# Streamed weights split by transfers: a rounding one for the first part, a negation on ACT, an adding one for the second

## The chip, the cores and the metric

The kernel runs on one core of a Trainium2 chip. The metric is the device time of one execution in microseconds (us), lower is better. Engines: TensorE (PE in the rows; PEld is its loading of weights), VectorE (DVE), ScalarE (ACT), GpSimd (POOL) and SyncE (SP), which issues transfers. SPq, POOLq and so on are the engines' queues.

## The reference

One step of a two-layer backbone with 512 latent and 128 context tokens, width 1024:

```
for l in range(2):
    mp, ms = modulation(c_ctx, ...), modulation(c, ...)     # silu(c) @ w_mod + b_mod, six parts
    h = rmsnorm(x, g_norm1) * (1 + m[1]) + m[0]
    qa, ka, va, qb, kb, vb, qc, kc, vc, gates = split(h @ w_in)     # 1024 -> 6912
    oa = diff_attention(...)            # 4 heads of two maps
    ob = gqa_attention(...)             # 8 heads on 2 key heads
    oc = neighbourhood_attention(...)   # 8 heads, latents; dense for the context
    y = g0 * (oa @ w_branch_a) + g1 * (ob @ w_branch_b) + g2 * (oc @ w_branch_c)
    x = x + m[2] * (y @ w_out)
    h2 = rmsnorm(x, g_norm2) * (1 + m[4]) + m[3]
    x = x + m[5] * (square(relu(h2 @ w_ff1)) @ w_ff2)       # 1024 -> 4096 -> 1024
y = rmsnorm(x, g_final)
```

Everything is float32; the new keys and values of the context are returned too.

## The kernel before

All 640 tokens stand as columns in on-chip memory. A float32 product is computed as three products of the faster fp32r type: both operands are split into a first part (rounded to fp32r) and a second (what is left), and first x first, first x second and second x first are summed. The two halves of the tokens are 256 and 384 columns (`HALVES`), so a block of 128 x 128 weights takes six matmuls.

**Stages of a layer.** First ten *units* of the mixer (`Unit`, u = 0 to 3 kind A, 4 and 5 kind B, 6 to 9 kind C): a unit projects the tokens with eight pieces of 384 weight columns (five token tiles, eight pieces, three matmuls each: 120 matmuls) and does its attention, whose steps are interleaved with the next unit's projections. Then gates and branches (three times eight gate products and eight branch products), then the out projection (its last part token half by token half, with the norm behind it: `staggered`), then the MLP in groups of blocks (`ff1`, `ff2`, `ff1_pair`), whose hidden pairs use a product scheme with seven summands made from sums of weights.

**The weights** are one long stream in HBM (`_stream`), cut into items by `_program`: kind "n" (loads of 768 columns, used as pieces of 384), kind "m" (512 or 256 columns, the second MLP product) and kind "s" (the seven summands of a hidden pair, made by sums of four loads). `Stream.make` prepares items ahead of their use: a load by SP into `raws` (or `spare`), the first part by ACT (`act(hi, x, AF.Copy)`, a rounding copy), the second by a subtraction, on POOL while `self.lo` is "POOL" (the units, `pl.ptt`), on VectorE after (`tt`). Both parts lie in rings `whis` and `wlos` of 10 x 384 columns; a place is refilled after the last matmul that reads it. In the units `ws.hold` keeps all eight pieces of a unit until its last token tile, which leaves two places for the next unit.

**The order.** Nothing is issued as the program is written. `Plan` records every operation with its engine, an assumed duration and its dependencies; `Plan.schedule` then runs a list scheduler over the records (each engine takes the earliest written operation that is ready) and `Plan.issue` writes the engines' programs in that order, which is fixed from then on: an engine that waits holds up all that stands behind it in its queue. Recorded helpers all have one line each: L245 matmul, L248 transpose, L262 ACT, L267 most of DVE, L280 a fused DVE operation, L294 the modulation's dot products, L305 and L311 POOL's one- and two-operand operations, L317 SP's transfers. Names in the rows: mf and mr are the large memories of float32 and fp32r, psm the accumulators, U, U1A, U1B, U1C further memories, w the weight stream, wmod the modulation weights, ospill the spilled branch outputs.

Of the kernel before, what the change touches and what calls it, by code (L numbers as in the profile page):

```python
# [13 lines left out]
AF = mybir.ActivationFunctionType  # L14
ALU = mybir.AluOpType
# [33 lines left out]
def f32(ap):  # L49
    return ap.bitcast(F32)  # L50
# [7 lines left out]
class Plan:  # L58
# [211 lines left out]
    def tt(self, out, a, b, op):  # L270
        self.vec("tensor_tensor", out, (a, b), op)
# [41 lines left out]
    def dma(self, out, in_, keys_out=(), keys_in=()):  # L313
# [2 lines left out]
            nb *= c  # L316
        self.add("SP", 60, lambda R: self.nc.sync.dma_start(R(out), R(in_)), [out], [in_], keys_out, keys_in, nbytes=4 * nb)  # L317


class Slots:  # L320

# [140 lines left out]
def hybrid_plan(pl, a, mf, mr, view, psm, xspill, ospill):  # L462
    mm, tp, act, tt, ts, stt = pl.mm, pl.tp, pl.act, pl.tt, pl.ts, pl.stt
# [43 lines left out]
    class Banks:  # L507
        def __init__(self, ids, w=1):
            self.ids, self.w, self.i = ids, w, 0
# [25 lines left out]
    class Stream:  # L535
# [3 lines left out]
        def __init__(self):  # L539
            self.items = []  # L540
            off = 0
            home = False
            for kind, n in _program():
                if kind == "layer":
                    home = True
                elif kind == "n":
                    c = 0
                    while c < n:
                        w = min(CW, n - c)
                        for j in range(0, w, PW):  # L550
                            self.items.append(("n", off, w, j, min(PW, w - j), home))
                            home = False
                        off += P * w
                        c += w
                elif kind == "m":
                    self.items.append(("m", off, n, 0, n, False))
                    off += P * n
                else:
                    self.items.append(("s", off, 0, n, SW, False))
                    if n == 0:  # L560
                        off += 4 * P * SW
            self.raws, self.parts = Circle(3 * CW), Circle(10 * PW)
            self.made = self.cur = self.off = 0
            self.hold = None
            self.pieces, self.v0 = {}, {}
            self.lo = "DVE"
            self.sum1 = self.spare = None

        def load(self, off, w):
# [8 lines left out]
        def make(self, upto):  # L578
            while self.made < min(upto, len(self.items)):
                i = self.made  # L580
                kind, off, w, j, n, home = self.items[i]
                if home:
                    self.parts.home()
                end = self.parts.look(n) + n
                h = self.cur if self.hold is None else self.hold
                if h in self.v0 and end - self.v0[h] > self.parts.size:
                    assert i > self.cur
                    break
                if kind == "n":
                    if j == 0:  # L590
                        self.raw = self.load(off, w)
                    x = self.raw[:, j:j + n]
                elif kind == "m":
                    x = self.spare.get()[:, :n]
                    pl.dma(x, self.piece(off, n))
                else:
                    if j == 0:
                        self.q = [self.load(off + k * P * SW, SW) for k in range(4)]
                    q, s1 = self.q, self.sum1
                    if j == 2:  # L600
                        tt(s1, q[2], q[3], ALU.add)
                        tt(q[2], q[0], q[2], ALU.subtract)
                        tt(q[0], s1, q[0], ALU.subtract)
                    if j == 6:
                        tt(q[1], q[1], q[0], ALU.subtract)
                    x = (q[0], q[1], q[0], s1, q[2], q[3], q[1])[j]
                self.v0[i], b = self.parts.take(n)
                hi, lo = whis[:, b:b + n], wlos[:, b:b + n]
                act(hi, x, AF.Copy)
                if self.lo == "POOL":  # L610
                    pl.ptt(lo, x, f32(hi), ALU.subtract)
                else:
                    tt(lo, x, f32(hi), ALU.subtract)
                self.pieces[i] = (hi, lo)
                self.made += 1
# [10 lines left out]
    ws = Stream()  # L626
# [667 lines left out]
    for l in range(DEPTH):  # L1294
# [11 lines left out]
        n = 0  # L1306
        for u in range(NU):
            un = Unit(l, u, ph)
            un.cached()
            if l == 0 and u == 0:  # L1310
                for t in ORDER:
                    un.evacuate(first_z[t], t)
            else:
                ws.hold = ws.cur
                W = [ws.get(UW, 1) for _ in range(KT)]
                ws.hold = None
                for t in ORDER:
                    un.project(W, t)
            for job in un.jobs():
                jobs.append(job)  # L1320
                step(n)
                n += 1
# [395 lines left out]
```

## Time and profile before

| | |
|---|---|
| median of 3 runs | 2417.46 us (2413.13 to 2419.87) |
| profiled execution | 2413.36 us |
| its span, first to last instruction | 2411.3 us |
| granted TensorE clock, mean | 0.99 |
| TensorE busy | 2330.3 us (97%) |
| VectorE / ACT / POOL busy | 1854.2 / 1227.5 / 445.3 us |
| moved by transfers | 245.39 MB |

Busy time is the time in which an engine executes something; waiting and issuing of transfers don't count. The rows below come from one execution, the profiled one. In a row of groups, the first figures are the busy time and the mean duration of one, and behind the second bar stands how long the engine was idle just before them and what ended it.

### The profile page before, as it was taken

How to read it: one execution, taken by the hardware profiler on the slowest of the kernel's cores; microseconds unless marked ns; L12 is line 12 of the kernel's file. 1: busy time of each engine (PE TensorE's matmuls, PEld its weight loads, DVE VectorE, ACT ScalarE, POOL GpSimd, SP SyncE). 2: the span in 40 equal slices, each digit the busy share in tenths (PEclk: the TensorE clock that was granted, in tenths of full speed). 3: DMA queues.
4: the chain of work that ended last, by engine and by line, in shares of the span. 5: the costliest groups of instructions: out<-in, count | busy, mean ns of one | idle time of the engine just before them, and what ended most of it. 6: DMA issues, size and time to landing. Idle time of an engine off the chain costs nothing. (4 is left out here: it accounts for less than half of the span.)

```text
span 2411.3 us, 42109 instructions
## 1 busy us (share of the span) xinstructions
PE 2330.3 (97%) x15460; PEld 2257.2 (94%) x15460; DVE 1854.2 (77%) x4067; ACT 1227.5 (51%) x2838; POOL 445.3 (18%) x527
## 2 busy tenths in 40 slices
PE   7898999999999899999999999999999999999997
PEld 5798999999999899999989998999999999999997
DVE  6878878789746999877787787777983688767777
ACT  4556677642233644444476567775222364444443
POOL 4636533300000000000034455431000000000000
PEclk8999999999999999999999999999999999999999
DMA  6211112476422244322241112226662212322222
GB/s 243 88 49 59 52 46 87 130 234 220 137 77 72 66 140 131 103 82 84 75 134 55 51 48 66 66 93 223 205 201 80 77 53 75 85 83 80 80 75 66
DMA packets 107346, 245.39 MB, mean 102 GB/s; under 512 B 13058, under 2 KB 26882, under 8 KB 106116
## 3 DMA queue, kind: packets, MB, share of 16 engines
q1 hardware_dynamic: 107140, 242.71, 32.6%
q8 instruction: 121, 1.98, 0.3%
q14 instruction: 85, 0.70, 0.1%
HBM read 225.62 MB, written 17.04 MB: 101 GB/s over the span
## 5 line engine op out<-in xcount | busy, mean ns | idle before, releaser
L245 PE MATMUL psm<-mr 128*128 128x256 f32 (+2 forms) x10688 | 1792.4, 319 | 21.0 <-ACT mr L262 8.8
L245 PEld LDWEIGHTS psm<-mr 128*128 128x128 f32 x10688 | 1640.6, 189 | 32.3 <-ACT mr L262 12.0
L262 ACT ACTIVATE mr<-mf 128x384 fp32r<-128x384 f32 (+4 forms) x948 | 470.6, 516 | 661.6 <-PE psm L245 576.9
L267 DVE TENSOR_TENSOR mr<-mf,mr 128x384 fp32r<-128x384 f32 (+5 forms) x780 | 432.1, 566 | 166.2 <-ACT mr L262 161.4
L280 DVE SCALAR_TENSOR_TENSOR mf<-psm,mf 128x256 f32<-128x256 f32 (+2 forms) x628 | 228.1, 408 | 92.9 <-PE psm L245 83.0
L311 POOL TENSOR_TENSOR mr<-mf,mr 128x384 fp32r<-128x384 f32 (+1 forms) x168 | 188.9, 1144 | 474.0 <-ACT mr L262 466.4
L262 ACT ACTIVATE mf<-mf 128x320 f32<-128x320 f32 (+6 forms) x417 | 195.9, 489 | 97.3 <-DVE mf L267 51.8
L311 POOL TENSOR_TENSOR mf<-mf 128x256 f32<-128x256 f32 (+3 forms) x93 | 89.9, 967 | 826.8 <-DVE mf L267 806.1
L294 DVE CUSTOM_DVE_ANT_0 psm<-mf,U1B 128x1024 f32<-128x1024 f32 x160 | 198.6, 1241 | 17.0 <-DMA mf<-wmod 15.8
L305 POOL TENSOR_SCALAR mf<-mf 128x640 f32<-128x640 f32 (+3 forms) x236 | 144.7, 617 | 350.9 <-DVE mf L267 284.1
L262 ACT ACTIVATE mf<-psm,mf 128x640 f32<-128x640 f32 (+3 forms) x256 | 162.4, 643 | 65.8 <-DVE mf L267 48.3
L245 PE MATMUL psm<-U,mr 128*128 128x320 f32 (+1 forms) x1176 | 186.4, 305 | 5.2 <-ACT U L262 4.0
L245 PEld LDWEIGHTS psm<-U,mr 128*128 128x128 f32 x1176 | 173.5, 188 | 6.9 <-ACT U L262 4.6
L267 DVE TENSOR_REDUCE mf<-psm 128x1 f32<-128x640 f32 (+2 forms) x212 | 148.4, 704 | 38.2 <-PE psm L245 32.7
L267 DVE TENSOR_TENSOR mr<-psm,mr 128x512 fp32r<-128x512 f32 (+2 forms) x252 | 141.1, 579 | 24.1 <-ACT mr L262 21.6
L245 PE MATMUL psm<-U1A,mr 128*128 128x384 f32 (+2 forms) x820 | 157.5, 313 | 2.1 <-DVE mf L280 2.1
L262 ACT ACTIVATE mr<-psm 128x512 fp32r<-128x512 f32 (+2 forms) x252 | 123.5, 513 | 52.4 <-PE psm L248 44.6
L267 DVE TENSOR_TENSOR mf<-mf 128x1 f32<-128x1 f32 (+8 forms) x265 | 138.0, 529 | 8.4 <-POOL mf L305 5.9
L245 PEld LDWEIGHTS psm<-U1A,mr 128*128 128x128 f32 x820 | 134.6, 191 | 2.6 <-DVE mf L280 2.6
L267 DVE TENSOR_TENSOR mf<-psm,mf 128x128 f32<-128x128 f32 (+5 forms) x248 | 93.2, 391 | 42.1 <-ACT mf L262 22.2
L248 PE MATMUL psm<-mf 128*128 128x128 f32 x752 | 119.9, 275 | 4.6 <-DVE mr L267 2.7
L267 DVE TENSOR_TENSOR mf<-mf,psm 128x320 f32<-128x320 f32 x196 | 95.0, 484 | 26.4 <-PE psm L245 24.7
(95 smaller groups left out, 1717.2 us busy)
## 6 DMA issues: line engine op xcount, KB each, us to landing
mf<-w SPq DMA_DIRECT2D x212, 384.0 KB, 3.2
mf<-w SPq DMA_DIRECT2D x170, 256.0 KB, 2.6
mf<-wmod SPq DMA_DIRECT2D x84, 512.0 KB, 4.0
U1C<-w SPq DMA_DIRECT2D x56, 256.0 KB, 2.7
mf<-bias SPq DMA_DIRECT2D x8, 1024.0 KB, 5.3
U<-wmod SPq DMA_DIRECT2D x12, 512.0 KB, 5.4
mf<-x SPq DMA_DIRECT2D x16, 320.0 KB, 7.0
ospill<-mf SPq DMA_DIRECT2D x16, 256.0 KB, 3.3
```

Source lines behind the costliest of these rows:

```text
L245: self.add("PE", d, lambda R: self.nc.tensor.matmul(R(out), R(lhsT), R(rhs), start=start, stop=stop), [out], [lhsT, rhs])
L248: self.add("PE", 55 if in_.dtype == F32R else 108, lambda R: self.nc.tensor.transpose(R(out), R(in_), ident), [out], [in_, ident])
L262: self.add("ACT", d, lambda R: self.nc.scalar.activation(R(out), R(in_), func, **kw), outs, ins)
L267: self.add("DVE", d, lambda R: getattr(self.nc.vector, name)(R(out), *map(R, ins), *args, **kw), [out] + list(extra), list(ins) + [x for x ...
L280: self.add("DVE", d, lambda R: self.nc.vector.scalar_tensor_tensor(R(out), R(a), s, R(b), op0, op1), [out], [a, b] + ([s] if hasattr(s, "a ...
L294: self.add("DVE", d, lambda R: self.nc.vector.tensor_tensor_reduce(out=R(out), in0=R(a), in1=R(b), scale=1.0, scalar=0.0, op0=ALU.mult, op ...
L305: self.add("POOL", d, lambda R: self.nc.gpsimd.tensor_scalar(R(out), R(a), s1, s2, op0, op1), [out], [a] + [s for s in (s1, s2) if hasattr ...
L311: self.add("POOL", d, lambda R: self.nc.gpsimd.tensor_tensor(R(out), R(a), R(b), op), [out], [a, b])
```

## The change

From the first unit on, items of kinds "n" and "m" are no longer loaded to `raws` by SP. POOL issues two transfers from the weight stream for each: one straight into the first part's place, whose type fp32r makes it a rounding one, and, after ACT has written the negative of that first part into the second part's place, one that adds the weight to it. The subtraction goes. The flag is set in the loop over the units and never set back; the first unit's eight pieces and one more are made before it, as before, and so are the summands "s" throughout. The scheduler gets 1000 ns for such a transfer's issue on POOL, and its usual terms for the landing.

```
+    def pdma(self, out, in_, add=False):
+
+        nb = 1
+        for _, c in out.ap:
+            nb *= c
+        kw = {"accum_op": ALU.add} if add else {}
+        self.add("POOL", 1000, lambda R: self.nc.gpsimd.dma_start(R(out), R(in_), **kw), [out], [in_] + ([out] if add else []), nbytes=4 * nb)
...
+            self.direct = False
...
-                if kind == "n":
+                if kind != "s" and self.direct:
+                    x = None
+                elif kind == "n":
...
+                if x is None:
+                    d = self.piece(off, w)[:, j:j + n]
+                    pl.pdma(hi, d)
+                    act(lo, f32(hi), AF.Copy, scale=-1.0)
+                    pl.pdma(lo, d, True)
+                    self.pieces[i] = (hi, lo)
+                    self.made += 1
+                    continue
...
             un = Unit(l, u, ph)
+            ws.direct = True
             un.cached()
```

In the built program POOL has 1094 transfers (547 rounding, 547 adding) and 152 subtractions fewer, VectorE 395 subtractions fewer, SP 337 transfers fewer; ACT and TensorE have as many instructions as before. The scheduler orders every engine anew. Three places:

TensorE, in the first layer's units, around the products with the values of a unit of kind A (`U_...,mr 128x256`); `mr 128x384` are projections of the next unit, `128x320` scores. Before:

```order
L245 MATMUL psm<-mr 128x384 x5
L245 MATMUL psm<-U_4_78_510,mr 128x256
L245 MATMUL psm<-mr 128x384
L245 MATMUL psm<-U_4_78_510,mr 128x256
L245 MATMUL psm<-mr 128x384 x2
L245 MATMUL psm<-U_4_78_510 128x320 x4
L245 MATMUL psm<-mr 128x384 x27
```

With the change:

```order
L245 MATMUL psm<-mr 128x384 x5
L245 MATMUL psm<-U_4_78_514,mr 128x256
L245 MATMUL psm<-mr 128x384 x4
L245 MATMUL psm<-U_4_78_514 128x320 x4
L245 MATMUL psm<-mr 128x384 x12
L245 MATMUL psm<-U_4_78_514 128x320 x4
L245 MATMUL psm<-mr 128x384 x12
```

The 27 projections that stood in one run now stand in smaller runs, with scores between them.

POOL, in the first layer's units, at the pieces of a next unit, with the semaphores that each waits for (DMASW: an earlier transfer of POOL's; PE: the last reader of the place; Activation: the negation; DMAHW: a transfer of SP's). A row that waits for PE is a rounding transfer, one that waits for Activation an adding one. Before:

```order
L311 TENSOR_TENSOR mr_64<-mf_63,mr_64 128x384 [waits DMAHW3_49,Activation_49]
L311 TENSOR_TENSOR mr_64<-mf_63,mr_64 128x384 [waits Activation_49]
L311 TENSOR_TENSOR mr_64<-mf_63,mr_64 128x384 [waits DMAHW7_49,PE_49,Activation_49]
L305 TENSOR_SCALAR mf_63<-mf_63 128x640 [waits DVE_49]
```

With the change:

```order
L325 DMA mr_64<-w 128x384 [waits DMASW2_49,PE_49]
L325 DMA mr_64<-w 128x384 [waits DMASW3_49,PE_49]
L325 DMA mr_64<-w 128x384 [waits DMASW4_49,PE_49]
L325 DMA mr_64<-w 128x384 [waits DMASW5_49,PE_49]
L325 DMA mr_64<-w 128x384 [waits DMASW6_49,Activation_49]
L325 DMA mr_64<-w 128x384 [waits DMASW7_49,Activation_49]
L325 DMA mr_64<-w 128x384 [waits DMASW0_49,Activation_49]
L305 TENSOR_SCALAR mf_63<-mf_63 128x640 [waits DVE_49,PE_49]
L325 DMA mr_64<-w 128x384 [waits DMASW1_49,Activation_49]
```

Where one subtraction stood for a piece there are now four rounding transfers in a row, then four adding ones, with the attention's row scaling (128x640) among them.

POOL, in the first layer from the branches to the MLP; `mr<-U`, `mr<-U1A` and `mr<-U1C` are the first parts of the spilled branch outputs, `128x2` and `128x3` the power in the norm of either token half. Before:

```order
L305 TENSOR_SCALAR mr<-U_8_98_4844 128x640 x4
L305 TENSOR_SCALAR mr<-U1A_103_4696 128x640 x3
L305 TENSOR_SCALAR mr<-U1C_108_4702 128x640 x3
L305 TENSOR_SCALAR mr<-U_8_98_4844 128x640 x2
L311 TENSOR_TENSOR mf<-mf 128x2
L311 TENSOR_TENSOR mf<-mf 128x3
```

With the change:

```order
L325 DMA mr<-w 128x384 x44
L305 TENSOR_SCALAR mr<-U1A_103_4714 128x640 x3
L305 TENSOR_SCALAR mr<-U1C_108_4721 128x640
L325 DMA mr<-w 128x384 x64
L305 TENSOR_SCALAR mr<-U1C_108_4721 128x640 x2
L305 TENSOR_SCALAR mr<-U_8_98_4873 128x640 x2
L325 DMA mr<-w 128x384 x96
L311 TENSOR_TENSOR mf<-mf 128x2
L325 DMA mr<-w 128x384 x13
L311 TENSOR_TENSOR mf<-mf 128x3
```

POOL's few operations of this stage now stand between long runs of transfers, the two powers among them.

## Rows read from the trace of the kernel before

**Rows 1.** The page, busy us, share of the span and instructions of each engine.

```profile
PE 2330.3 (97%) x15460; PEld 2257.2 (94%) x15460; DVE 1854.2 (77%) x4067; ACT 1227.5 (51%) x2838; POOL 445.3 (18%) x527
```

**Rows 2.** Stretches: length, busy us (xinstructions) of PE, PEld, DVE, ACT, POOL, clock, DMA share, GB/s.

```profile
0.00:100.00 100.00, 76.25 (x391) 59.15 (x392) 73.87 (x144) 45.49 (x111) 49.34 (x47) 0.88 0.53 185
100.00:490.00 390.00, 375.53 (x2461) 353.57 (x2461) 302.52 (x755) 261.48 (x691) 167.39 (x212) 1.00 0.24 76
490.00:780.00 290.00, 290.00 (x1988) 289.91 (x1987) 206.37 (x395) 90.25 (x178) 12.77 (x13) 1.00 0.46 143
780.00:860.00 80.00, 73.89 (x475) 71.51 (x475) 76.02 (x179) 49.15 (x108) 2.71 (x1) 0.98 0.30 88
860.00:1220.00 360.00, 360.00 (x2462) 360.00 (x2461) 296.00 (x610) 173.07 (x345) 3.52 (x4) 1.00 0.35 100
1220.00:1300.00 80.00, 72.70 (x435) 65.92 (x435) 63.88 (x147) 54.38 (x136) 35.71 (x38) 1.00 0.34 108
```

**Rows 3.** Waits of TensorE over the span: us in total, times, longest us.

```profile
PE psm L245 <- ACT mr L262: 9.6, 10, 3.2
...
PE psm L245 <- POOL mr L311: 5.5, 5, 2.4
```

**Rows 4.** Groups by line and shape over the span: busy us, mean ns.

```profile
L311 POOL TENSOR_TENSOR mr<-mf,mr 128x384 fp32r<-128x384 f32 x161 | 175.5, 1109 | 461.5 <-ACT mr L262 454.0 <-DVE mf L267 6.9
L267 DVE TENSOR_TENSOR mr<-mf,mr 128x384 fp32r<-128x384 f32 x293 | 162.7, 562 | 125.1 <-ACT mr L262 122.6 <-PE psm L245 1.2
L262 ACT ACTIVATE mr<-mf 128x384 fp32r<-128x384 f32 x450 | 228.3, 522 | 371.1 <-PE psm L245 334.4 <-DMA mf<-w 17.3 <-DVE mr L267 7.2
L311 POOL TENSOR_TENSOR mr<-mf,mr 128x640 fp32r<-128x640 f32 x7 | 13.7, 1954 | 12.5 <-ACT mr L262 12.4
L305 POOL TENSOR_SCALAR mf<-mf 128x640 f32<-128x640 f32 x96 | 78.2, 814 | 178.1 <-DVE mf L267 122.4 <-PE psm L245 25.2 <-PE psm L248 13.0
```

**Rows 5.** Groups in 490 to 780 us, the split on DVE.

```profile
L267 DVE TENSOR_TENSOR mr<-mf,mr 128x384 fp32r<-128x384 f32 x107 | 59.6, 562 | 58.6 <-ACT mr L262 58.1
```

**Rows 6.** Groups of DVE in 780 to 860 us.

```profile
L267 DVE TENSOR_TENSOR mr<-mf,mr 128x384 fp32r<-128x384 f32 x16 | 8.8, 553 | 1.1 <-ACT mr L262 0.9
L267 DVE TENSOR_TENSOR mr<-mf,mr 128x512 fp32r<-128x512 f32 x12 | 8.1, 679 | 0.0
```

**Rows 7.** The weight stream as a tile: SP's issues in ns, min/median/max, and landing.

```profile
L317 SPq DMA_DIRECT2D mf<-w x390: 327/328/1442, 11.9 to 2363.1; - x195
...
DMA to landing us min/median/max: 2.0/2.9/8.9
```

**Rows 8.** Transfers by issuing line: KB each, median us to landing.

```profile
mf<-w SPq DMA_DIRECT2D x170, 256.0 KB, 2.6
...
U<-wmod SPq DMA_DIRECT2D x12, 512.0 KB, 5.4
```

**Rows 9.** Groups of POOL in 100 to 490 us.

```profile
L311 POOL TENSOR_TENSOR mr<-mf,mr 128x384 fp32r<-128x384 f32 x63 | 66.6, 1076 | 18.5 <-ACT mr L262 18.3
```

**Rows 10.** Timeline near 171 us, a run of projections: start us, us.

```profile
171.47 4.85 PE L245 MATMUL psm<-mr 128*128 128x384 f32 x27
```

**Rows 11.** Groups of POOL in 490 to 860 us, the longer of the norm's powers.

```profile
L311 POOL TENSOR_TENSOR mf<-mf 128x3 f32<-128x3 f32 x1 | 2.7, 2707 | 15.0 <-DVE mf L267 15.0
```

**Rows 12.** Waits of POOL over the span: us in total, times, longest us.

```profile
POOL mr L305 <- DMA U<-ospill: 30.9, 3, 15.9
```

**Rows 13.** DMA queues: packets, MB, share of 16 engines' span.

```profile
q1 hardware_dynamic: 107140, 242.71, 32.6%
```

**Rows 14.** Groups of DVE over the span, the largest groups that scale or cast from SBUF to SBUF.

```profile
L267 DVE TENSOR_SCALAR U1B<-U1B 128x1024 f32<-128x1024 f32 x4 | 4.3, 1082 | 0.0
...
L267 DVE CAST U1A<-mf 128x384 fp32r<-128x384 f32 x4 | 1.4, 355 | 0.0
```

**Rows 15.** A stretch of 20 us, columns as in rows 2.

```profile
820.00:840.00 20.00, 15.87 (x92) 14.51 (x92) 20.00 (x47) 9.53 (x20) 0.00 (x0) 0.93 0.25 78
```

## The prediction

> **What bounds the kernel now.** I read the busy table first: TensorE works 2330.3 of 2411.3 us, so all that any change of the other engines can win is the 81 us in which it does not [rows 1]. The stretches by stage then say where these lie [rows 2]. In 490 to 780 us (gates, branches) and 860 to 1220 us (MLP) TensorE is busy without a gap, at 1988 matmuls in 290 us, 0.146 us each; nothing done to the weights' preparation can shorten these 650 us, nor their twins in the second layer. The gaps are in the start (23.8 us of the first 100), in the ten units of the mixer (14.5 us in 100 to 490), at the passage from out projection to MLP (6.1 us in 780 to 860; I take the second layer's as equal), at the layer's end (7.3 us in 1220 to 1300) and at the tail. The waits of TensorE confirm it: the split of the streamed weights holds it up for at most 9.6 us behind ACT and 5.5 us behind POOL, over the whole span [rows 3]. So the change takes work from engines that are not the bound; the question is what it puts in its place.
>
> **Removed.** 395 subtractions on VectorE and 152 on POOL go (547 pieces), and 337 loads leave SP's queue. A piece of 384 columns costs DVE 0.56 us and POOL 1.11 us [rows 4], one of 512 columns costs DVE 0.68 us [rows 6]. That is at least 395 x 0.56 = 221 us of DVE and 169 us of POOL, nearly all beside TensorE's work. ACT keeps as many instructions, of the same size (0.52 us for 384 columns); they now negate the first part instead of rounding the raw weight. In 490 to 780 us the 107 DVE subtractions [rows 5] leave an engine that is 206 us busy out of 290: worth 0. Where they can count is the passage to the MLP: there DVE is 76.0 of 80 us busy, and 28 of its instructions are such splits, 16.9 us [rows 6], a few of the wide ones belonging to the summands, which stay. I take 12 us off DVE there. TensorE's idle time in the three passages is 6.1 + 6.1 + 7.3 = 19.5 us; some of it is the latency of the norm itself, so I take half, **-10 us**; the bounds are 0 and -19.5.
>
> **Added: 1094 transfers on POOL's queue.** No row shows a transfer issued by POOL. The price of an issue is bounded below by SP's, 0.33 us [rows 7], and above by the longest mean of POOL's tensor instructions, 1.95 us (128x640) [rows 4]. Between them I take 1.1 us, the row of POOL over the same 128x384 tile. For landing I take 2.6 us after the issue, the row of the 256 KB weight loads [rows 8], since these pieces are 192 and 256 KB; the longest landing of a weight load was 8.9 us [rows 7].
>
> In the gates and branches a piece feeds three column blocks of 128, each of them three products in two halves: 18 matmuls, 2.63 us. POOL must issue two transfers in that time. In 490 to 780 us that is 2 x 107 x 1.1 + 12.8 (what POOL does there now) = 248 of 290 us: POOL becomes 86% busy and TensorE stays the bound. **The tipping point is (290 - 12.8) / 214 = 1.30 us an issue.** In the MLP a step has 36 matmuls, 5.3 us, for two transfers: far from it. So both cost 0, hidden under TensorE; if an issue takes 1.95 us, the first stretch grows by 140 us in each layer. The ring of ten pieces is 26 us deep there, and a piece needs about 1.1 + 2.6 + 0.5 + 1.1 + 2.6 = 7.9 us from slot to use, so latency alone is hidden too.
>
> In the units it isn't as free. Eight of the ten ring places are held by the running unit, so the next unit's pieces are made as the last projection releases them. Before: ACT 0.52, then POOL 1.08 each [rows 9]: first piece 1.6 us after release, eighth 9.2 us. Now POOL issues in groups, four roundings and then the four adds that wait for ACT (the order's second place): first piece 4 x 1.1 + 1.1 + 2.6 = 8.1 us, eighth 16 x 1.1 + 2.6 = 20.2 us. That is 6.5 to 11 us later in each of 18 units. What covers it: 63 pieces passed in 390 us, so a unit lasts 49 us, of which its 120 projection matmuls are 120 x 0.18 = 22 us [rows 10]; 27 us of attention matmuls can stand in between, and the order's first place shows that they do. The cover ends when attention itself waits: its row scalings (0.81 us each [rows 4]) now queue on POOL behind transfers that wait for TensorE or ACT. Per unit the cost lies between 0 and 11 us; the nearest row is the present gap, 14.5 us in eight units, 1.8 us each. I let it grow by half, 1 us: **+18 us**. POOL is 167.4 - 66.6 + 126 x 1.1 = 239 of 390 us busy there, so it is not full.
>
> At a norm, POOL's power (up to 2.7 us [rows 11]) stood alone; it now queues between transfers (the order's third place), each of which may first wait for a ring place. One issue for each of two half norms at three passages: 6 x 1.1 = **+6 us**; bounds 0 and 6 x 2.63.
>
> POOL's scalings of the spilled branch outputs come between transfers too, and one of them waited 15.9 us for its load at the first gates [rows 12]; transfers behind it wait along. The filled ring holds 10 x 2.63 = 26 us of work for TensorE at that moment, so I cost it at 0; with an empty ring it would be 15.9 us a layer. SP's other loads only come earlier, which nothing waits for.
>
> **Transfers' load.** The hardware queue moved 242.7 MB in 32.6% of sixteen engines' span [rows 13], 309 GB/s when busy. A second reading of 113.6 MB adds 15 points; if the add's reading of its own destination counts, 30. In 490 to 780 us the share is 0.46; weights are 75 GB/s of the 143, so it goes to 0.70, or 0.95 at the upper bound. I cost that at 0; an excess would show as late landing.
>
> Two statements of pages speak against the change. VectorE's largest groups of scalings and casts from one SBUF tile to another are 4.3 and 1.4 us in the whole span [rows 14]. By the Trainium skill, "SBUF — State Buffer", section "Who interferes with whom", such an instruction may hold a port pair that POOL needs to write descriptors, so the sum would be up to 5.7 us higher; no row here shows such a stall. By the Trainium skill, "DMA: Bandwidth & Descriptors", section "Latency and other measured facts", a transfer from GpSimd brings its first byte about 1 us after issue against 0.6 us from SP; an estimate from this page is 2 x 0.4 x 18 = 14 us more where nothing covers it.
>
> **The sum**: -10 + 18 + 6 = +14 us on the profiled execution's 2413.4 us, 2427 us. The runs' median, 2417.5, lies 4.1 us above that execution, so I expect 2431 us.
>
> **Rivals.**
> 1. *POOL becomes the bound.* The add reads two streams and may take longer to issue than the rounding; past 1.30 us in the mean, the gates starve. For it: no row excludes it, and 86% is near. Against it: 1.1 us is the cost of a whole pass over the tile, and an issue touches no data. At 1.5 us, 2 x 107 x 1.5 + 12.8 = 334, 44 us over in each layer; in the units 16 x 0.4 = 6.4 us later, half covered, 18 x 3.2 = 58. With the forecast's +14: 2417.5 + 160 = 2578 us. Chance 0.21.
> 2. *Faster.* The mechanism is DVE at the passages, where it is the busiest engine (20.00 of 20 us in 820 to 840 [rows 15]), and the cover in the units holds. It decides if POOL's issue is well under 1.1 us, so that neither units nor norms lose. It gives two thirds of 19.5, 13 us: 2404 us. Against it: the norm's own chain (power, row scaling, ACT) is as long as before. Chance 0.28.
> 3. *Late landing.* If the adding transfer lands at about 5.4 us, the row of a 512 KB load [rows 8], the chain grows by 5.6 us; the MLP's ring (7.5 pieces of 512 columns, some 16 us) still covers 14 us, but in the units half of it stays, 18 x 2.8 = 50 us: 2482 us. Chance 0.13.
> That the flag does less than it says is excluded by the order: all pieces but the first nine and the MLP's summands become transfers, because it is set in the first unit and never reset.
>
> **Numbers.** The forecast has 0.38. A measurement tells about 0.3% from no change, 7.3 us: 2410 to 2425 counts as same. The forecast's own range, with 0 to 3 us a unit and 0 to -19 at the passages, is 2404 to 2460: of its 0.38, 0.04 is faster, 0.12 same, 0.22 slower. Rival 2 gives 0.23 faster and 0.05 same; rivals 1 and 3 are slower, 0.34. Together 0.27 faster, 0.17 same, 0.56 slower. The range from 2402 to 2578 leaves out a part of rival 2 and the half of rival 1 with longer issues, about 0.19.
>
> **What would show it.** Right: POOL's transfers near 1.1 us; TensorE still 290 of 290 us in the gates; POOL near 86% there; TensorE's gaps in the units a little longer; DVE below 65 of 80 us at the passages with a shorter gap. Wrong: gaps in the gates (TensorE waiting for transfers or POOL), or units of 49 us grown by more than 3 us.

## The result and the profile after

The change makes the kernel slower: 2482.75 us median (2478.84 to 2486.08) against 2418.18 (2413.13 to 2419.87) for the kernel before, a ratio of 1.0259, interval [1.0242, 1.0276]. That is 64.6 us; the prediction said 13.5 (2431 us), with this result inside its range.

The page of the changed kernel, busy time of each engine, POOL's DMA queue (packets, MB, share of 16 engines' span) and the groups of the new transfers and of the negation:

```profile
PE 2361.2 (95%) x15460; PEld 2269.2 (91%) x15460; DVE 1630.7 (66%) x3672; ACT 1225.9 (49%) x2838; POOL 1060.1 (43%) x1469
...
q0 software_dynamic: 157536, 227.22, 48.0%
...
L325 POOL DMA_DIRECT2D mr<-w x1094 | 795.0, 901 | 1089.4 <-PE psm L245 502.0
L262 ACT ACTIVATE mr<-mr 128x384 fp32r<-128x384 f32 (+2 forms) x547 | 289.2, 540 | 498.6 <-DMA mr<-w 466.8
```

VectorE lost 224 us (1854.2 [rows 1] to 1630.7), as the prediction counted (at least 221), and TensorE gained nothing from it: it is busy for 31 us longer with the same 15460 matmuls, and idle for 41 us longer. POOL's queue carries 227 MB at 48.0% of the engines' time. That is 227.22 MB / (0.48 x 2483.0 us) = 191 GB/s, against 309 for SP's queue before [rows 13].

The times from issue to landing, on the page (KB each, median us):

```profile
mr<-w POOLq DMA_DIRECT2D x834, 192.0 KB, 5.0
mr<-w POOLq DMA_DIRECT2D x224, 256.0 KB, 4.3
mf<-wmod SPq DMA_DIRECT2D x84, 512.0 KB, 6.2
```

SP's weight loads of 256 KB took 2.6 us [rows 8].

**Where the time went.** I divide a run into four stages by SP's transfers: the units of a layer end with the first (second layer: the last) reload of `ospill` into U1A, the first layer with the first store to `xspill`, the second with the first store to `y`. Stretches of the kernel before (columns as in rows 2):

```profile
0.00:478.90 478.90, 440.80 (x2773) 402.17 (x2774) 368.97 (x884) 299.81 (x786) 215.06 (x257) 0.97 0.29 93
478.90:1218.30 739.40, 733.16 (x4989) 730.27 (x4988) 584.11 (x1189) 318.49 (x644) 19.29 (x20) 1.00 0.39 119
1218.30:1650.10 431.80, 414.30 (x2669) 386.44 (x2668) 337.26 (x843) 291.14 (x769) 191.94 (x234) 1.00 0.25 77
1650.10:2392.90 742.80, 736.58 (x5009) 733.57 (x5008) 551.56 (x1126) 315.85 (x637) 18.19 (x17) 1.00 0.35 104
```

and of the changed one:

```profile
0.00:496.10 496.10, 447.93 (x2764) 400.38 (x2765) 349.17 (x871) 299.34 (x781) 250.62 (x342) 0.97 0.51 119
496.10:1246.80 750.70, 739.50 (x4997) 734.69 (x4996) 493.09 (x1003) 316.89 (x649) 292.44 (x407) 0.99 0.77 173
1246.80:1712.30 465.50, 427.79 (x2663) 393.77 (x2662) 316.72 (x833) 292.85 (x764) 227.43 (x325) 0.98 0.49 105
1712.30:2464.80 752.50, 740.64 (x5017) 735.62 (x5016) 459.46 (x940) 314.62 (x643) 288.77 (x398) 1.00 0.72 158
```

The units (first and third row, the start included) take 17.2 and 33.7 us longer, 50.9 together; the rest of the layers 11.3 and 9.7, 21.0 together. In the units TensorE's idle time grew from 55.6 to 85.9 us (length less busy time), and its busy time by 20.6 us for a few matmuls less.

Nearly all of the rest's 21 us are lost in the gates and branches. Two stretches of equal length from the start of this stage, before and after, in the first layer:

```profile
479.00:783.00 304.00, 303.87 (x2083) 303.37 (x2082) 216.63 (x417) 99.51 (x199) 14.34 (x16) 1.00 0.47 149
496.00:800.00 304.00, 298.33 (x2023) 295.41 (x2023) 159.14 (x284) 90.52 (x186) 170.60 (x238) 0.99 0.96 221
```

and in the second:

```profile
1650.00:1948.00 298.00, 297.87 (x2044) 297.25 (x2044) 210.34 (x403) 95.36 (x189) 14.78 (x15) 1.00 0.48 150
1712.00:2010.00 298.00, 290.56 (x1966) 287.20 (x1965) 156.05 (x279) 89.08 (x182) 170.18 (x235) 1.00 0.96 222
```

With the change 60 and 78 matmuls fewer pass. At the 0.146 us of a matmul in this stage before, that is 8.8 and 11.4 us, some 20 together.

The second layer's units at close range (columns as in rows 2) show how idle and longer busy time belong together:

```profile
1260.00:1270.00 10.00, 7.54 (x34) 6.73 (x34) 5.15 (x12) 6.90 (x17) 3.58 (x4) 0.83 0.77 160
1270.00:1280.00 10.00, 7.15 (x45) 6.89 (x46) 8.14 (x22) 8.84 (x23) 1.72 (x2) 1.00 0.00 0
...
1340.00:1350.00 10.00, 7.05 (x31) 6.48 (x31) 5.50 (x14) 4.46 (x14) 5.42 (x7) 0.83 0.56 79
1350.00:1360.00 10.00, 10.00 (x68) 9.69 (x67) 8.74 (x22) 6.76 (x17) 1.94 (x3) 1.00 0.07 25
```

TensorE sits idle for 2.5 to 3 of 10 us; in two of these stretches the granted clock is 0.83 in the mean, a part of them at the lower level of 1.2 GHz, and 31 to 34 matmuls pass where 68 pass in the full one. So a gap costs the idle time and, at some gaps, slower matmuls too.

What TensorE's weight loads waited for in these units (us in total, times, longest), first before, 1220 to 1650 us:

```profile
PEld psm L248 <- DVE mr L267: 15.3, 26, 1.8
PEld psm L248 <- ACT mr L262: 4.1, 11, 0.7
PEld psm L245 <- ACT mr L262: 3.7, 6, 1.2
PEld psm L245 <- ACT mf L262: 2.4, 5, 0.7
```

then after, 1248 to 1712 us:

```profile
PEld psm L245 <- ACT mf L262: 12.6, 11, 3.4
PEld psm L245 <- DMA mr<-w: 12.5, 15, 2.3
PEld psm L248 <- DVE mr L267: 11.0, 22, 1.1
PEld psm L248 <- ACT mr L262: 6.3, 13, 1.2
```

About half of the new waiting is for weights (`mr<-w`, 12.5 us). Nearly as much (12.6 - 2.4 us) is for ACT's results in `mf`, which are attention's own. My reading is that these are steps that before had projections beside them.

### The profile page after: what moved, and what is told of

Same layout as the page of the kernel before. It is cut to its first block, busy times and chain, and to the rows that moved or that the text cites. A ratio compares the mean times of both kernels' runs of the same rounds, so it can differ in the third digit from the quotient of the medians.

```text
span 2483.0 us, 42915 instructions
## 1 busy us (share of the span) xinstructions
PE 2361.2 (95%) x15460; PEld 2269.2 (91%) x15460; DVE 1630.7 (66%) x3672; ACT 1225.9 (49%) x2838; POOL 1060.1 (43%) x1469
## 3 DMA queue, kind: packets, MB, share of 16 engines
q0 software_dynamic: 157536, 227.22, 48.0%
## 4 chain that ended last, share of the span: by engine, by line
PE 66%; issue 9%; DMA 8%; POOL 6%; DVE 6%; ACT 5%; POOLq 0%; ACTq 0%; DVEq 0%; SPq 0%
PE psm L245 62%; DMA mr<-w 6%; POOL mr L325 5%; PE psm L248 4%; ACT mr L262 2%; DVE mf L267 2%; DVE mr L267 2%; DMA mf<-wmod 2%; ACT mf L262 1%; DVE mf L280 1%; POOL mf L311 1%; DVE psm L294 1%; ACT U L262 1%; DVE U L267 1%; POOL mr L311 0%
## 5 line engine op out<-in xcount | busy, mean ns | idle before, releaser
L325 POOL DMA_DIRECT2D mr<-w x1094 | 795.0, 901 | 1089.4 <-PE psm L245 502.0
L262 ACT ACTIVATE mr<-mr 128x384 fp32r<-128x384 f32 (+2 forms) x547 | 289.2, 540 | 498.6 <-DMA mr<-w 466.8
L262 ACT ACTIVATE mr<-mf 128x512 fp32r<-128x512 f32 (+5 forms) x465 | 224.9, 500 | 261.8 <-PE psm L245 232.2
L267 DVE TENSOR_TENSOR mr<-mf,mr 128x512 fp32r<-128x512 f32 (+5 forms) x449 | 234.7, 531 | 56.1 <-ACT mr L262 54.0
L294 DVE CUSTOM_DVE_ANT_0 psm<-mf,U1B 128x1024 f32<-128x1024 f32 x160 | 198.1, 1238 | 78.0 <-DMA mf<-wmod 75.9
L267 DVE TENSOR_TENSOR mf<-mf 128x512 f32<-128x512 f32 (+8 forms) x265 | 125.6, 482 | 12.5 <-ACT mf L262 8.3
```

Of the source, the lines that this page charges most:

```text
L262: self.add("ACT", d, lambda R: self.nc.scalar.activation(R(out), R(in_), func, **kw), outs, ins)
L267: self.add("DVE", d, lambda R: getattr(self.nc.vector, name)(R(out), *map(R, ins), *args, **kw), [out] + list(extra), list(ins) + [x for x ...
L294: self.add("DVE", d, lambda R: self.nc.vector.tensor_tensor_reduce(out=R(out), in0=R(a), in1=R(b), scale=1.0, scalar=0.0, op0=ALU.mult, op ...
L325: self.add("POOL", 1000, lambda R: self.nc.gpsimd.dma_start(R(out), R(in_), **kw), [out], [in_] + ([out] if add else []), nbytes=4 * nb)
```

## The experiments

Theories for the units' 51 us: **CHAIN/LATE**, the pieces come late after a ring place is released; **QUEUE**, POOL's waiting transfers hold up attention's operations behind them; **ORDER**, the scheduler, told that pieces come late, arranges TensorE's program worse. All runs are timed beside the kernel before (medians 2417 to 2421 us in the six sessions). The stage figures are from the profiled executions, against the 2413.4 us one of before, which lies 4 to 8 us under those medians; so their sums differ from the differences of the medians by up to that and by each run's own scatter.

| run | median us | ratio [interval] | units, both layers | rest, both layers |
|---|---|---|---|---|
| the change | 2482.75 | 1.0259 [1.0242, 1.0276] | +50.9 | +21.0 |
| e1_units_only | 2465.86 | 1.0183 [1.0168, 1.0198] | +51.1 | +0.3 |
| e2_rest_only | 2428.61 | 1.0031 [1.0021, 1.0041] | +2.1 | +13.6 |
| e3_no_add | 2446.20 | 1.0099 [1.0082, 1.0116] | +40.9 | -5.2 |
| e4_round_only | 2453.15 | 1.0129 [1.0114, 1.0144] | +33.4 | +5.6 |
| e7_order | 2488.57 | 1.0283 [1.0266, 1.0301] | +56.6 | +19.9 |
| e8_quick | 3704.70 | 1.5282 [1.5230, 1.5335] | +253.1 | +1040.5 |
| e9_dve | 2456.51 | 1.0154 [1.0129, 1.0178] | +50.3 | +0.7 |
| e5_told | 2476.88 | 1.0238 [1.0221, 1.0255] | +60.7 | +3.5 |
| e10_ring12 | 2430.81 | 1.0055 [1.0035, 1.0075] | +9.5 | +4.6 |
| e12_ring12_dve | 2420.39 | 1.0016 [1.0000, 1.0031] | +7.7 | -2.7 |
| e13_ring12_mix | 2417.80 | 0.9998 [0.9985, 1.0012] | +4.1 | +1.4 |
| e14_other_order | 2411.92 | 0.9967 [0.9958, 0.9976] | -2.6 | +2.2 |
| e15_told_issue | 2487.30 | 1.0284 [1.0269, 1.0300] | +30.7 | +42.7 |
| e16_told_landing | 2479.27 | 1.0248 [1.0231, 1.0265] | +32.8 | +34.3 |
| e17_mix_dve | 2426.55 | 1.0031 [1.0019, 1.0043] | +13.3 | +1.1 |
| e18_told_none | 2463.49 | 1.0191 [1.0167, 1.0215] | +5.7 | +38.1 |
| e19_order_loads | 2504.20 | 1.0357 [1.0334, 1.0380] | +58.3 | +35.6 |

**By place: e1 and e2.** The flag is set only in the units, or only after them.

```
e1:          ws.lo = "DVE"
+            ws.direct = False
e2:  -           ws.direct = True       (in the units; set behind ws.lo = "DVE" instead)
```

> The weights are split by transfers only in the ten units of each layer; gates, branches, out projection and MLP are as in the kernel before. In the changed kernel the units fell behind by 17 us in the first layer and by 34 us in the second, the rest by 11 and 10 us. Theory LATE (the transfers of POOL's queue land after 5.0 us where 2.6 us were reckoned, so the chain from a free ring place to a usable piece is longer; in the gates they fill the DMA engines) and rival QUEUE (attention's scalings stand on POOL behind transfers that wait) both keep the units' loss: 2418 + 45 to 55 us. If the units' loss in the second layer is an effect of the rest being late, it is below 40 us.

> The units are as in the kernel before; gates, branches, out projection and MLP are split by transfers. LATE: the gates keep a DMA share near 1 and lose 8 to 10 us a layer, in all 2418 + 15 to 25 us. QUEUE: POOL has hardly any other work there, so nothing is queued behind a transfer but the norm's power; 2418 + 0 to 6 us.

The units' loss appears with transfers in the units, the rest's with transfers in the rest. Most of the loss is made in the units. e1's time lies in the range of its theories; e2's lies between its two ranges.

**By kind: e3 and e4.** e3 leaves out the addition of the second transfer, which then writes the rounded weight where the second part belongs; e4 keeps the rounding transfer and goes back to a load and a subtraction for the second part.

```
e3:  -  pl.pdma(lo, d, True)
     +  pl.pdma(lo, d)
e4:  -  act(lo, f32(hi), AF.Copy, scale=-1.0)
     -  pl.pdma(lo, d, True)
     +  x = (raw weights, loaded by SP)
     +  pl.ptt(lo, x, f32(hi), ALU.subtract)       (tt where ws.lo is "DVE")
```

> Leaves the addition out: the second transfer writes the rounded weight over the negated first part, so the second part is not what is left of the weight. Same number of transfers, same waits, same order on every engine. LATE with the adding transfer as its cause: landing of POOL's transfers falls from 5.0 us to 3.5 us or less, the DMA share in the gates falls from 1.0 to 0.75 or less, time 2435 to 2450 us. LATE with the rounding (type change) as its cause: landing stays at 4.5 us or more, 2475 to 2485 us. QUEUE: POOL's issues stay, so 2475 to 2485 us as well, with landing short.

> The first part comes by the rounding transfer; the raw weight is loaded by SP as before and the second part is a subtraction on POOL (units) or DVE (rest) as before; ACT's work on the pieces is gone. Bytes from HBM as in the changed kernel. LATE by the adding transfer: 2415 to 2430 us, landing of the rounding ones 3 us or less. LATE by the rounding: 2445 us or more. QUEUE: POOL issues one transfer and one subtraction for a piece in the units, about as long as two transfers, so the units keep most of their 51 us: 2455 us or more.

TensorE's instructions stand in e3's units in the very order of the change, since the scheduler is told the same. So e3 shows what the addition itself costs: 2482.8 - 2446.2 = 36.6 us, by stages 10.0 in the units and 26.2 in the rest. Its page, POOL's queue and the landings:

```profile
q0 software_dynamic: 157536, 227.22, 36.0%
...
mr<-w POOLq DMA_DIRECT2D x834, 192.0 KB, 3.0
```

The same 227 MB take 36.0% instead of 48.0% of the engines' time, and a piece lands after 3.0 instead of 5.0 us. Issue, as rows of the weight stream (ns, min/median/max), in the change, then in e3:

```profile
L325 POOL DMA_DIRECT2D mr<-w x1094: 530/877/2609, 1.3 to 2451.4; - x183
```

```profile
L325 POOL DMA_DIRECT2D mr<-w x1094: 527/535/850, 1.3 to 2414.1; - x183
```

Without additions an issue is 0.535 us on POOL. In the change the trace tells the kinds apart by what they wait for: two rounding transfers that waited for PE, and two adding ones that waited for ACT (start us, us of both):

```profile
109.81 1.17 POOL L325 DMA_DIRECT2D mr<-w  x2 [1.03 <-PE psm L245]
114.78 1.83 POOL L325 DMA_DIRECT2D mr<-w  x2 [0.39 <-ACT mr L262]
```

Over the whole trace of the change, the 534 that wait for ACT have a median issue of 0.89 us, none under 0.84. The others (13 adding ones that don't wait among them) have 0.56 us and land after 3.0 where no adding one is in flight (161), but 0.88 and 5.0 where one is (399). So the addition makes the rounding transfers beside it slower too. (The busy time, 795.0 us, gives 0.73 a transfer: durations overlap.) In the gates, the change and then e3 (columns as in rows 2):

```profile
500.00:600.00 100.00, 99.67 (x678) 98.77 (x677) 66.63 (x104) 31.25 (x64) 57.53 (x79) 1.00 1.05 277
600.00:700.00 100.00, 96.51 (x651) 95.25 (x650) 58.55 (x103) 28.07 (x58) 57.77 (x82) 1.00 1.00 235
```

```profile
500.00:600.00 100.00, 99.67 (x680) 98.82 (x679) 71.34 (x112) 34.58 (x71) 50.01 (x85) 1.00 0.98 295
600.00:700.00 100.00, 100.00 (x684) 100.00 (x683) 52.37 (x93) 28.07 (x59) 45.03 (x82) 1.00 0.83 227
```

With the addition the DMA engines are full, share 1.0 for 200 us; without it (0.98 and 0.83, more than the 0.75 that was expected) TensorE runs through. What TensorE's weight loads wait for there, with the change, 500 to 800 us:

```profile
PEld psm L245 <- ACT U1A L262: 3.9, 4, 2.6
PEld psm L245 <- DVE U1A L280: 2.1, 2, 1.8
PEld psm L245 <- DMA mr<-w: 0.8, 1, 0.8
```

and ACT, same stretch:

```profile
ACT mr L262 <- DMA mr<-w: 190.0, 66, 8.3
```

It is seldom the weights themselves. ACT stands for 190 of 300 us waiting to negate pieces that have not landed, and the gates' activations (`U1A`), for which TensorE waits longest, stand behind in its queue. But 41 of the units' 51 us stay without the addition, and 33 in e4. e4's time is in the range that would blame the rounding (2445 us or more), though its pieces of 192 KB land after 3.4 us, not 5.0. So a slow landing isn't most of what the units lose.

**Order or delay: e7 and e8.** e7 gives before's work the change's order: the scheduler sees the transfers with their costs, the engines get the loads, copies and subtractions of before. e8 is the reverse: the change's transfers, told as free (rounding) or as a subtraction (adding).

```
e7:  pl.pdma(hi, d)          ->  POOL 1000 ns and landing in the plan, nothing issued
     act(lo, f32(hi), ...)   ->  act(hi, x, AF.Copy)
     pl.pdma(lo, d, True)    ->  POOL 1000 ns and landing in the plan, issued as ptt(lo, x, f32(hi), subtract)
     (x: loaded by SP, in the plan free of cost)
e8:  pl.pdma(hi, d)          ->  0 ns and no landing in the plan
     pl.pdma(lo, d, True)    ->  the subtraction's ns and no landing in the plan
```

> The order that the scheduler made for the change (it is told the two transfers with their costs), but the work of before: loads by SP, a rounding copy on ACT, the subtraction; no transfer on POOL's queue. Three theories for the part of the units' loss that stays when the addition is left out (41 of 51 us in both layers). ORDER (the rearranged instructions themselves cost it): 2455 to 2465 us, units 13 and 28 us longer than before. CHAIN (the pieces come later after a ring place is released, whatever the order) and QUEUE (POOL's waiting transfers hold up attention's operations behind them): 2415 to 2430 us, units within 5 us of before.

> The work of the change, but the scheduler is told that a rounding transfer takes nothing and an adding one as long as the subtraction, with no landing, so that the order is made as for before's work. ORDER: the units fall back to within 10 us of before and only the rest's 21 us stay, 2435 to 2445 us. CHAIN or QUEUE: the delay is there and nothing is laid over it, units at least as long as with the change (+51 us), 2480 to 2560 us.

ORDER came true for the units, and more than the 41 us that it had: +56.6 us with no transfer of POOL's at all. The total lies above every range; the rest, which I come back to at e18, is part of that. (Of TensorE's instructions in the first layer's units, 96% stand in e7 as with the change, in the second layer's over 99%; between before and the change it is 57% and 35%.) In e7, 1252 to 1720 us, TensorE's weight loads waited for attention:

```profile
PEld psm L245 <- ACT mf L262: 18.6, 16, 4.4
PEld psm L248 <- DVE mr L267: 12.4, 24, 1.1
```

e8 shows that the order isn't a mere mistake: with quick pieces planned for, the kernel takes 3705 us, far beyond both ranges, at a mean granted clock of 0.84 (0.99 before). Its waits over the span:

```profile
ACT mr L262 <- DMA mr<-w: 1704.1, 386, 8.4
POOL mr L325 <- ACT mr L262: 1692.3, 426, 7.9
```

In the rest, where 1040 us of it are lost, rounding and adding transfers then alternate on POOL's queue (98% of neighbours are of different kinds, about 70% with the change), and an adding one that waits 4.0 us for the landing and the negation (1692.3 / 426) holds back the next piece's rounding one.

**QUEUE and true costs: e9 and e5.** e9 moves attention's scalings and small additions in the units from POOL to VectorE (`pl.pts` to `ts`, one `pl.ptt` to `tt`). e5 tells the scheduler what was measured (issue 900 ns, 190 GB/s, landing 1800 ns instead of 700).

> The change, with attention's scalings and its small additions in the units on VectorE instead of POOL (the powers stay on POOL). QUEUE: these no longer stand behind transfers that wait for a ring place, so at least half of the units' 51 us goes, 2445 to 2460 us. CHAIN or ORDER: 2475 to 2490 us.

> The change, with the scheduler told what was measured: 900 ns for an issue, 190 GB/s for POOL's transfers, 1800 ns instead of 700 for their landing. ORDER (it was misled by its costs): an order made with true costs gives back half of the units' loss, 2450 to 2465 us. CHAIN: later pieces are now planned for, but no order can take away the wait for them: 2475 to 2490 us.

e9's total fell in QUEUE's range, but not where QUEUE says: its units are as long as the change's (+50.3 to +50.9; by layer +24.4 and +25.9 against +17.2 and +33.7). Of the 26 us between the medians, 20.3 show in the rest, whose instructions e9 doesn't touch; only the order was made anew, and with it the rest's loss went from 21.0 to 0.7 us though the adding transfers stay. (e9's profiled execution lies 7.8 us above its median, so this split is rough.) So QUEUE isn't what the units lose by, and the rest's loss depends on the order by some 20 us. e5's total is in CHAIN's range and its units are no shorter (+60.7): told true costs, the scheduler finds no better order.

**Look-ahead: e10, e12, e13, and the control e14.** In the units the raw loads' memory is idle after the change. Moved into it, the rings hold 12 pieces, so that four of a unit's eight, not two, can be made before the running unit lets go.

```
-  whis, wlos = perr.tile(10 * PW), perr.tile(10 * PW)
+  whis, wlos = perr.tile(12 * PW), perr.tile(12 * PW)
```

e12 adds e9's move to VectorE; e13 uses transfers only in the units and for the MLP's second product. e14 is the kernel before with POOL's subtraction told at 1.08 us instead of 0.98.

> The change with rings of 12 pieces instead of 10, in the memory that its raw loads no longer need (the first nine pieces are loaded in pieces of 384, the summands' loads lie in three small corners). Four pieces of a unit instead of two can then be prepared before the running unit releases a place. CHAIN (the pieces come late after a release, and the order was made for late pieces): the units give back about half of their 51 us, 2450 to 2465 us. ACCIDENT (another order costs what it costs, whatever the reason for it): nothing can be said of the units, 2470 to 2495 us as good as any.

> The same rings of 12, and attention's scalings on VectorE as in the run before with rings of 10, which took 2456.5 us. If both gains are real they add: units within 30 us of before's, the rest within 5 us, 2420 to 2440 us. If the first gain was an accident of the order: as the ring of 12 alone, 2450 to 2465 us.

> The rings of 12; transfers of POOL only in the units and for the second product of the MLP, loads and VectorE's subtraction in gates, branches, out projection and the first product. The adding transfers no longer fill the DMA engines in the gates: the rest within 5 us of before, and the units as with the ring of 12 alone: 2430 to 2450 us if CHAIN holds, 2460 to 2470 us if the ring does nothing.

> A control: the kernel before, with POOL's subtraction told to the scheduler at 1.08 us (what the trace shows) instead of 0.98 us, so that it makes another order of the same work for no reason of the change. ACCIDENT: an order is worth tens of microseconds either way, 2390 to 2450 us. CHAIN: within 8 us of before, 2410 to 2426 us.

e10 wins back 52 us, 41 of them in the units, more than the half that was expected, with the same told costs and landings of the same kind. Its waits in the second layer's units, 1220 to 1660 us:

```profile
PEld psm L248 <- DVE mr L267: 10.5, 21, 1.2
PEld psm L245 <- DVE mf L267: 8.3, 6, 5.0
PEld psm L248 <- ACT mr L262: 6.9, 16, 0.7
PEld psm L245 <- DVE mf L280: 5.5, 4, 2.6
PEld psm L245 <- ACT mf L262: 2.3, 3, 0.9
```

The wait for `mr<-w` is gone from the top, and the one for ACT's `mf` is back at before's 2.4. e13 ends level with the kernel before, though in its second layer's units TensorE waits 10.0 us for `mr<-w`; they lose 4.4. e14 shows that another order for no reason moves the total by 8 us, and the units by 2.6. But 90% of TensorE's instructions in its first layer's units stand as before, so it is a mild control; e18 below has another order too (71%) and loses 5.7 us in the units. ACCIDENT is too small for 51. Adding e9's move to e13 as well:

> Rings of 12, transfers of POOL only in the units and for the MLP's second product, and attention's scalings on VectorE. If the 10 us that the scalings gave with rings of 12 are not an accident of the order, 2405 to 2412 us, below both kernels; otherwise 2415 to 2425 us.

It lost 9 us, so the gain in e12 can't be put down to the scalings; a new order weighs as much. No version with transfers is faster than the kernel before.

**What the order reacts to: e15, e16 and their controls e18, e19.** e15 is e7 told the issues but no landing, e16 told the landing but one issue, e18 told neither, e19 is e7 with its loads told as SP's.

> Before's work in an order for which the scheduler was told only the two issues of 1 us on POOL's queue for each piece, with nothing for their landing. If the landing is what it arranges the units badly for, this loses little: 2418 to 2435 us. If the occupied queue is, 2455 to 2490 us.

> Before's work in an order for which the scheduler was told the landing of both transfers (2.6 us each) and one issue of 1 us, as the subtraction's, so that POOL's queue is as occupied as before. If the landing is what it arranges the units badly for: 2455 to 2490 us. If the occupied queue is: 2418 to 2435 us. If only both together, both runs stay below 2440 us.

> A control for the two runs before: built in the same way (before's work; loads that the scheduler sees as free; the subtraction on POOL), but told neither the issues nor the landing. If those runs show the order that the told costs make, this one has the units within 10 us of before in both layers, and 2415 to 2435 us in all. If the way of building costs it, the units are again 30 us or more longer, 2450 to 2490 us, and the runs with told costs say nothing of the change.

> The change's costs told, before's work, and the loads told as SP's with their bytes and landing. ORDER: the units are 35 us or more longer than before again, 2450 to 2490 us. If the free loads of the earlier run were its cause: units within 10 us, 2415 to 2435 us.

I judge these by the units alone, because e18 shows that the way of building costs 38 us in the rest (there the subtraction is POOL's, not VectorE's); I hadn't foreseen that, and it spoils the totals that were expected, also e7's. The units with the same work: +5.7 told neither, +30.7 told the issues, +32.8 told the landing, +56.6 and +58.3 told both. Each adds some 26 us, and e7 less e18 is 50.9, the change's own loss. That they agree so closely is in part luck: the change also pays 10 us in the units for the addition (e3). Neither expectation, that one of the two is the cause, was right. e19's order isn't the change's either (63% and 76% of TensorE's instructions in the two layers' units stand as there), so the loss hangs on what was told and not on one unlucky order. How a worse order costs its time is shown only in part: in e7, e3 and the change TensorE waits in the second layer's units for attention's `mf` (18.6, 15.7 and 12.6 us, against 2.3 in e18), but in e16, which loses 20 us there, that wait is 2.1 us.

## Why the prediction was right and wrong

- **Bound and direction: right.** TensorE remained the bound; nothing that left VectorE was worth much.
- **The units, "I let it grow by half, 1 us: +18 us": the step that failed.** It measured 50.9 us, 2.8 for each of 18 units, within the bounds of 0 to 11. The chain, 6.5 to 11 us later, was hardly the error: with the measured 0.90 us an issue and 5.0 from issue to landing, the same working gives 4 x 0.9 + 5.0 = 8.6 and 15 x 0.9 + 5.0 = 18.5 us, 7 to 9 us later than before, because the issue was put too long and the landing too short (an estimate; no run measures the chain as such). The order's smaller runs were read as proof that attention's 27 us cover it. They were the cost: before's work in that order, with no transfer to wait for, loses 56.6 us in the units (e7), 50.9 more than its control (e18), and two more ring places give 41 back (e10). I read it so: a projection that is planned late is missing beside attention's steps elsewhere, and TensorE waits there for attention. The cover isn't free time; it was already in use.
- **Gates at 0, "hidden under TensorE": the second step that failed.** Some 20 of the rest's 21.0 us are lost there, where the sum has 0. POOL was no bound: 0.73 us of busy time a transfer, POOL 57.5 of 100 us busy, not 86, so rival 1 fell. But the upper bound for the DMA engines, 0.95, was the true reading (0.96 over the stage, with 1.05 and 1.00 in its first 200 us), and the excess did come out as late landing, through ACT. The addition is needed for it (e3: -5.2 us in the rest), but not enough: in other orders the same additions cost next to nothing there (e9: +0.7). Why, stays open.
- **Landing, "I take 2.6 us after the issue": wrong choice.** 5.0 us for 192 KB; the row of the plain load told nothing of an adding transfer (3.0 without the addition). Rival 3 held this: landing near 5.4 us, 50 us more in the units, 2482 us. That its total is the measured one is luck: it adds its 50 us to the forecast's 18, so it has 68 in the units and -4 for all else, where 50.9 and +21.0 were measured. Its mechanism is a part of it: e3 has quick landings in the same order and keeps 41 us in the units, and e15 and e16 put as much on the two issues as on the landing.
- **Passages, -10 us: too much.** The first one, before and after (columns as in rows 2):

```profile
783.00:873.00 90.00, 83.89 (x546) 81.51 (x545) 84.32 (x193) 54.95 (x119) 2.71 (x1) 0.98 0.29 86
```

```profile
800.00:890.00 90.00, 85.31 (x547) 83.94 (x546) 79.74 (x189) 56.34 (x127) 27.66 (x38) 0.96 0.62 127
```

  VectorE has 4.6 us less to do, not 12. TensorE's idle time fell from 6.1 to 4.7 us, but its busy time rose by as much, at a granted clock of 0.96 instead of 0.98: 546 and 547 matmuls pass in the same 90 us. VectorE's groups in these two stretches, before (the 16 of 384 columns have the row of [rows 6] there) and then after, show what was counted wrongly:

```profile
L267 DVE TENSOR_TENSOR mr<-mf,mr 128x512 fp32r<-128x512 f32 x16 | 10.9, 680 | 0.0
```

```profile
L267 DVE TENSOR_TENSOR mr<-mf,mr 128x512 fp32r<-128x512 f32 x9 | 6.2, 686 | 0.0
...
L267 DVE TENSOR_TENSOR mr<-mf,mr 128x384 fp32r<-128x384 f32 x10 | 5.6, 555 | 1.5 <-ACT mr L262 1.5
```

  19 of the 32 splits of these shapes are still there: they aren't the stream's, but the summands' and the tokens' own. So 7.9 us went, and other work of VectorE's moved into the stretch. Rival 2 rested on this gain and fell.
- **Norm's power, +6:** not measured by itself. The first passage, with its powers in it, is neither longer nor shorter than before.
- **The page on DMA latency** (the Trainium skill, "DMA: Bandwidth & Descriptors", section "Latency and other measured facts": 1 us against 0.6 to the first byte) isn't contradicted by e3: 3.0 us for 192 KB from POOL, 2.6 for 256 KB from SP [rows 8]; no run shows a first byte. The stall of descriptors by VectorE shows in no row: in e3 no issue took over 0.85 us. (The prediction's 4.3 us wasn't VectorE's largest group of that kind; `mf<-mf 128x2` has 4.7.)

## What to carry to other kernels

Before lengthening the way by which a tile gets ready, count how many tiles may be in preparation at once: if most places of the ring are held, added microseconds shift the work that used to cover other waits, as here, and a scheduler's plan shows this as filler in smaller runs. Look for the memory that the change frees, and spend it on look-ahead first (two more places were worth 52 us here). To part a new order from a new cost, run the old work in the new order, with a control built in the same way and told nothing.

## What the runs showed that was not expected

- An adding transfer on POOL's queue issues in 0.89 us against 0.535 for a plain or rounding one, and a rounding one takes 0.88 while an adding one is in flight. With both in the mix the queue moves 191 GB/s while busy; without the addition 227.22 MB in 36.0% of 2447.5 us are 258 GB/s.
- With the DMA engines at share 1.0 others land later too: the modulation weights' 512 KB, 4.0 us to landing before and 4.5 in e3, took 6.2, and VectorE waited 75.9 us for them (15.8 before, 39.4 in e3).
- Two transfers of a piece that alternate on one in-order queue, the second waiting for the first's result, made the kernel 1.53 times as long (e8); with transfers of the first kind issued ahead, as in the change (four before four of the second in the units, seven at the start of the rest), the same transfers cost 2.6%.
- A list scheduler's order of the same work, changed by 0.1 us in one told cost, moved the time by 0.33% (e14).
